# Two value groups of a decoder layer computed as one group of 1024 features

## The chip, the core and the metric

The kernel is one launch on one core of a Trainium2 chip. The metric is device time in microseconds (us) of the whole launch. Engines: PE is TensorE (matmuls), DVE is VectorE, ACT is ScalarE, POOL is GpSimd, SP is SyncE, which here issues most of the weight loads. DMAs can be issued from SP, ACT and POOL; those from SP and ACT go by the chip's hardware queues, those from POOL by a software queue.

## The reference

One layer of a decoder: 512 tokens, width 1024, float32. After an RMS norm, one input projection `h @ w_in` feeds two token mixers: gated linear attention (q, k, v, gate) and dilated attention in three groups of four heads with head width 128. The groups have dilations 1, 4 and 16, and their outputs are merged with weights made from their softmax sums:

```
for g, (win, dil) in enumerate(ATT_GROUPS):
    o_g, lse_g = dilated_attention(q_g, k_g, v_g, bias_g, dil, win // dil)
wts   = softmax(stack(lses), axis=0)
o_att = sum(wts[..., None] * stack(outs), axis=0)
```

Then come two merge gates, the output projection, an MLP with squared relu, and a gated projection of a side input. The change touches only the value projections of groups 1 and 2 (each 1024 x 512, here called v1 and v2), which need the tokens ordered by class: token t modulo 4.

## The kernel before, in words

**Precision and operands.** Every large product is made of three matmuls in a float32 form that TensorE takes rounded: hi x hi, hi x lo, lo x hi. A weight operand is a tile of 128 partitions x 1024; ACT rounds it to `hi` (L244), DVE subtracts to get `lo` (L239). Both tiles are padded, and those of the products below start at an offset of 32 elements (`SHIFT`).

**Products.** A projection of 512 features is done by Winograd's form of Strassen's scheme (`strassen`, L295 on): seven products of half size instead of eight. Its weight operands are A11, A12, A22 as loaded and S1 = A21 + A22, S2 = S1 + A11, S3 = A11 + A21, S4 = S2 + A12. S1 and S3 are made by a DMA that accumulates onto a loaded tile, issued by POOL (L210, L221; S3 over A11's tile, in place); S2 and S4 are DVE sums (L218, L224). For values the token tile is the stationary side and the weights are the moving side, 256 columns in each matmul; a product is four row pairs x two token halves x three matmuls = 24, so one group has 7 x 24 = 168 matmuls. Each product runs in one PSUM bank. After products 0 to 3 ACT copies a bank out (`begin`, L332); at the end DVE adds a later bank to that copy (`add`, L350).

**What sets the order.** Instructions are written out in program order, and every engine runs its own in that order. `fetch` keeps the preparation of operands a fixed number of operands ahead of the products: operand i+1 is rounded, i+2 summed, i+3 loaded (`prepare`), and S1's load and accumulation come 5 operands before A11 (`EARLY`). After every 8 matmuls `step` runs one queued evacuation from `later` and, when enough columns have passed (`pace`), one piece of a side generator from `side`. `drain` takes steps until both lists are empty, with no product between.

**Around the change.** While v1 and v2 run, the side generator `scores12` computes the scores of groups 1 and 2 (16 small matmuls for each of four heads, L704 and L705; softmax L683, L684, exponentials L688). Then it writes the softmax statistics to DRAM and reads them back in token order (L717, L719, both on POOL's queue), and PE transposes them (L723). `values_cls` brings values into class order the same way: four stores to `v_dram` (L662) and four strided reads back (L668) for each group, on POOL's queue. After v2 there is a `drain`; then v0 runs with `weights` as side generator. This makes the merge weights, and moves them through DRAM too (`k_dram` L770, `cc` L771, POOL). Then gq runs with `pv` as side generator, which multiplies probabilities by `cc` (L787), transposes them (L807, copied out L799) and multiplies them by v0 (L813, L815) and by v1 and v2 (L823, L824).

```
w = raw[f"{q}.S1"] = load(f"{q}.A21")
GP.dma_start(w, wts[UNIT[f"{q}.A22"]], accum_op=OP.add)      # L210
w = raw[f"{q}.S3"] = raw[f"{q}.A11"]
GP.dma_start(w, wts[UNIT[f"{q}.A21"]], accum_op=OP.add)      # L221
```

Of the kernel before, what the change touches and what calls it, by code (L numbers as in the profile page):

```python
# [10 lines left out]
F32 = mybir.dt.float32  # L11
# [3 lines left out]
OP = mybir.AluOpType  # L15
# [4 lines left out]
P = 128  # L20
# [14 lines left out]
def att_col(g, which):  # L35
    return ATT + (g * 3 + which) * 512


QUADS = ("quad", "quadt")


MLP2 = (("plain", 0, 0), ("seven", 0, 1), ("seven", 1, 1), ("plain", 0, 2), ("seven", 0, 3), ("seven", 1, 3),
# [4 lines left out]
def weight_units():  # L47

    u = []

    def fm(name, src, col, n, row=0):
        for j in range(n):
            u.append((f"{name}.{j}", "fm", src, row, col + j * P))

    def tm(name, src, col):
        for i in range(4):
            u.append((f"{name}.{i}", "tm", src, i * 2 * P, col))

    def quad(name, src, col, kind="quad", chunk=0):
        for m, k in ((0, 0), (1, 0), (1, 1), (0, 1)):  # L60
            u.append((f"{name}.A{m + 1}{k + 1}", kind, src, 2 * chunk + k, col + m * (P if kind == "quad" else 256)))

    fm("k0", "w_in", att_col(0, 1), 4)
    fm("q1", "w_in", att_col(1, 0), 4)
    quad("k1", "w_in", att_col(1, 1))
    quad("q2", "w_in", att_col(2, 0))
    quad("k2", "w_in", att_col(2, 1))
    quad("v1", "w_in", att_col(1, 2), "quadt")
    quad("v2", "w_in", att_col(2, 2), "quadt")
    quad("v0", "w_in", att_col(0, 2), "quadt")  # L70
    quad("gq", "w_in", GQ)
    quad("gk", "w_in", GK)
    quad("gv0", "w_in", GV, "quadt")
    for j in range(4):
        u.append((f"oa.{j}", "half", "w_o_attn", 0, j * 2 * P))
    quad("r0", "w_in", GR)
    quad("gv1", "w_in", GV + 512, "quadt")
    quad("r1", "w_in", GR + 512)
    for i in range(2):
        quad(f"gb{i}", "w_in", GATE + D + i * 512)  # L80
    for i in range(2):
        quad(f"ga{i}", "w_in", GATE + i * 512)
    fm("og", "w_o_gla", 0, 8)
    fm("wo", "w_out", 0, 8)
    for q in range(8):
        quad(f"m1q{q}", "w_mlp1", q * 512)
    for what, sub, c in MLP2:
        if what == "plain":
            for kk in range(4 * c, 4 * c + 4):
                u.append((f"m2s{sub}.{kk}", "tm", "w_mlp2", kk * 2 * P, sub * 512))  # L90
        else:
            quad(f"m2s{sub}c{c}", "w_mlp2", sub * 512, chunk=c)
    for j in range(2):
        u.append((f"pp{j}.0", "tm", "w_pp", 0, j * 512))
    for j in range(2):
        tm(f"pg{j}", "w_pg", j * 512)
    return u
# [13 lines left out]
BEGIN = {0: (((0, 0), "a"),), 1: (((1, 1), "c"),), 2: (((1, 0), "d"),), 3: (((0, 1), "a"),)}  # L111
END = {4: (((0, 0), "b"),), 5: (((0, 1), "c"),), 6: (((1, 1), "a"), ((1, 0), "a"))}

LEAD = 5


def operand_order():

    names = []
    for name, kind, *_ in UNITS:  # L120
        if kind not in QUADS:
            names.append(name)
        elif name.endswith("A11"):
            names += [f"{name[:-3]}{a}" for a, _, _ in STAGES]
    return names


OPERANDS = operand_order()
OPERAND = {n: i for i, n in enumerate(OPERANDS)}

EARLY = {max(i - LEAD, 0): n[:-4] for n, i in OPERAND.items() if n.endswith(".A11")}

C_LN2, C_LN3, C_BA, C_GN, C_LN1, C_LO, C_N = 0, 8, 16, 20, 28, 36, 38
W0, W12 = 384, 256
# [13 lines left out]
def block_kernel(ctx, tc, xT, ws, pT, wts, wha, wa2, vec, lnf, rel, onehot, ident_d, mask_d, out):  # L148
# [50 lines left out]
    def load(name):  # L199
        w = wst.tile([P, 1024], F32, tag="w", name="w")  # L200
        SY.dma_start(w, wts[UNIT[name]])
        return w

    def prepare(i):

        name = OPERANDS[i]
        if i in EARLY:
            q = EARLY[i]
            w = raw[f"{q}.S1"] = load(f"{q}.A21")
            GP.dma_start(w, wts[UNIT[f"{q}.A22"]], accum_op=OP.add)  # L210
        if name in UNIT:
            raw[name] = load(name)

    def sums(i):
        q, _, what = OPERANDS[i].rpartition(".")
        if what == "S2":
            w = raw[f"{q}.S2"] = raw[f"{q}.S1"]
            V.tensor_tensor(w, w, raw[f"{q}.A11"], op=OP.add)  # L218

            w = raw[f"{q}.S3"] = raw[f"{q}.A11"]  # L220
            GP.dma_start(w, wts[UNIT[f"{q}.A21"]], accum_op=OP.add)  # L221
        elif what == "S4":
            w = raw[f"{q}.S4"] = raw[f"{q}.S2"]
            V.tensor_tensor(w, w, raw[f"{q}.A12"], op=OP.add)  # L224

    def split_weights(tag, i, bufs):

        t = wsp.tile([P, 1024 + PAD], F32R, tag=tag, name=tag, bufs=bufs)
        o = SHIFT if OPERANDS[i] not in UNIT or UNITS[UNIT[OPERANDS[i]]][1] in QUADS else 0
        return t[:, o:o + 1024]  # L230

    def fetch(upto):
# [22 lines left out]
    def run(mms, n=PIECE, shared=False):  # L255
        for i in range(0, len(mms), n):
            for o, l, r, a, b in mms[i:i + n]:
                TE.matmul(o, lhsT=l, rhs=r, start=a, stop=b, skip_group_check=shared)  # L258
            step(PIECE * r.shape[-1])

    def three(ps, pairs):

# [38 lines left out]
    def strassen(name, xo, finish, tm=False, scale=1.0, extra=None, acc=None):  # L301

        bank, sums = {}, acc or {}

        def stage(op, xname, b):
            wh, wl = weight(f"{name}.{op}")
            fresh = b not in bank
            if fresh:  # L310
                bank[b] = mmt()
            mms = []
            for pr in range(4):
                xh, xl = xo(xname, pr)
                for n in range(2):
                    o = bank[b][:, halves(n)]
                    if tm:
                        c, r = slice(n * P, (n + 1) * P), slice(pr * 256, (pr + 1) * 256)
                        three = ((xh[:, c], wh[:, r]), (xl[:, c], wh[:, r]), (xh[:, c], wl[:, r]))
                    else:  # L320
                        c = slice((2 * pr + n) * P, (2 * pr + n + 1) * P)
                        three = ((wh[:, c], xh), (wh[:, c], xl), (wl[:, c], xh))
                    for i, (l, r) in enumerate(three):
                        mms.append((o, l, r, fresh and not mms, pr == 3 and i == 2))
            run(mms, shared=True)

        def begin(c, b):
            def go():
                if acc:
                    return add(c[0], sums[c], sums[c], bank[b])  # L330
                sums[c] = u32()
                S.activation(sums[c], bank[b], AF.Copy, scale=-scale if c[0] else scale)  # L332
            later.insert(0, go)

        def end(c, b):
            later.append(lambda: finish(*c, sums[c], bank[b]))

        for i, s in enumerate(STAGES):
            stage(*s)
            for c, b in BEGIN.get(i, ()):  # L340
                begin(c, b)
            for c, b in END.get(i, ()):
                end(c, b)
            if extra:
                extra(i)

    def add(m, out, s, ps, scale=1.0):

# [293 lines left out]
    def values(name, parts=False):  # L642
# [9 lines left out]
        strassen(name, xs_op, finish, tm=True)  # L652
        return res

    def values_cls(name):

        v_dram = dr.tile([T, 512], F32, name="v_dram")
        res, left = [], [4]

        def finish(m, t, s, ps):  # L660
            add(m, s, s, ps)
            GP.dma_start(v_dram[t * HT:(t + 1) * HT, m * HT:(m + 1) * HT].rearrange("(n p) c -> p n c", n=2),  # L662
                         s.rearrange("p (n c) -> p n c", n=2))
            left[0] -= 1
            if not left[0]:
                for c in range(4):
                    v = u32()
                    GP.dma_start(v, v_dram.rearrange("(m c) f -> c m f", c=4)[c])  # L668
                    res.append(v)

        strassen(name, xs_op, finish, tm=True)
        return res

    def softmax(ps, n0, bias, nm, sums, col, prob):
# [17 lines left out]
    st12 = const.tile([P, 2, 16], F32, name="st12")  # L692
    st0 = const.tile([P, 2, 16], F32, name="st0")
    sn = const.tile([P, 2, 16], F32, name="sn")
    p12, p0 = [], []

    def scores12():
        for h in range(4):
# [15 lines left out]
            yield  # L714

        s_dram = dr.tile([8, T], F32, name="s_dram")
        GP.dma_start(s_dram.rearrange("r (m c) -> m r c", c=4), st12.rearrange("p s (h c) -> p (s h) c", c=4))  # L717
        s_row = u32()
        GP.dma_start(s_row[0:32, 0:P], s_dram.rearrange("r (b t) -> (r b) t", b=4))  # L719
        for _ in range(6):  # L720
            yield
        pst = smt()
        TE.transpose(pst[:, 0:32], s_row[0:32, 0:P], ident[0:32, 0:32])  # L723
        yield
        V.tensor_copy(sn.rearrange("p a b -> p (a b)"), pst[:, 0:32])

    def scores0():
        for h in range(4):
# [14 lines left out]
    def weights():  # L743

        def small(name):
            return st.tile([P, 16], F32, tag=name, name=name, bufs=1)

        nmx, e0, e1, e2, dn, cn1 = (small(n) for n in ("nmx", "e0", "e1", "e2", "dn", "cn1"))
        V.tensor_tensor(nmx, st0[:, 0, :], sn[:, 0, :], op=OP.min)
        V.tensor_tensor(e0, nmx, st0[:, 0, :], op=OP.subtract)  # L750
# [272 lines left out]
    drain()  # L1023
    side.append(scores12())
    pace[0] = 3072
    v1 = values_cls("v1")
    v2 = values_cls("v2")
    drain()
    pace[0] = 2048
    side.append(weights())  # L1030
    v0 = values("v0")
# [479 lines left out]
def _layout(inputs):  # L1511
# [3 lines left out]
    for i, (_, kind, s, r, c) in enumerate(UNITS):  # L1515
# [2 lines left out]
            a = w[r:r + D, c:c + P].reshape(8, P, P).transpose(1, 0, 2)  # L1518
        elif kind == "tm":
            a = w[r:r + 2 * P, c:c + 512].reshape(2, P, 512).transpose(1, 0, 2)  # L1520
        elif kind == "quadt":

            a = w.reshape(4, 2, P, -1)[:, r, :, c:c + 256].transpose(1, 0, 2)
# [46 lines left out]
```

## Time and profile before

| | us |
|---|---|
| median of three runs | 964.02 (963.95 to 965.0) |
| profiled execution | 964.0 |
| its span on the core | 962.2 |
| PE busy | 954.1 |
| DVE busy | 743.2 |
| ACT busy | 538.2 |
| POOL busy | 103.6 |

The profiled execution is the span and 1.8 us around it. Its time is that of the median, so sums made on the trace can be set against the median as they are. Times in the views count from the start of the span. In the trace v1's products begin at 141.27, v2's at 168.49, v0's at 188.83 and gq's at 208.88. A busy PE is no proof of PE at its peak: the time from one matmul's start to the next (here: the cadence) says how fast it runs, and a matmul's own duration, which overlaps the next one, does not.

### The profile page before, as it was taken

The numbers are of one execution on the slowest core, as the hardware profiler recorded it, in microseconds if no ns is written. First come the engines' busy times: TensorE is split into PE (matmuls) and PEld (weight loads), VectorE is DVE, ScalarE is ACT, GpSimd is POOL, SyncE is SP. The second block draws the span as 40 slices with busy tenths as digits, with TensorE's granted clock in tenths as the row PEclk, the third lists the DMA queues.
The fourth block names the chain that finished last, engine by engine and source line by source line (L and its number), as shares of the span: only waits on it lengthen the run. The fifth ranks groups of instructions, "written<-read, shape, count | busy, mean of one in ns | idle before, by whom it ended". The sixth has DMA issues, their size and how long they took to land.

```text
span 962.2 us, 16747 instructions
## 1 busy us (share of the span) xinstructions
PE 954.1 (99%) x6734; PEld 894.2 (93%) x6734; DVE 743.2 (77%) x1064; ACT 538.2 (56%) x880; POOL 103.6 (11%) x145
## 2 busy tenths in 40 slices
PE   9999999999999999999999999999999999999997
PEld 8789999999998999999988899999998998988886
DVE  7688879676788769978856788777677899787754
ACT  7357547445657666675833446556665674354633
POOL 0140001420001021013010000011000100000000
PEclk9999999999999999999999999999999999999999
DMA  9385564964446555556536437565654464553102
GB/s 325 118 237 122 136 152 114 256 200 116 110 119 186 155 123 141 128 137 197 155 100 205 117 79 196 135 151 159 174 154 110 115 182 102 134 195 106 45 1 88
DMA packets 41326, 138.92 MB, mean 144 GB/s; under 512 B 5347, under 2 KB 5935, under 8 KB 41248
## 3 DMA queue, kind: packets, MB, share of 16 engines
q1 hardware_dynamic: 27648, 93.27, 29.2%
q0 software_dynamic: 12160, 42.20, 22.2%
q10 hardware_dynamic: 1440, 2.38, 0.7%
q8 instruction: 53, 0.87, 0.4%
q14 instruction: 25, 0.20, 0.1%
HBM read 131.50 MB, written 8.17 MB: 145 GB/s over the span
## 4 chain that ended last, share of the span: by engine, by line
PE 98%; DVE 1%; issue 1%; ACT 0%; POOL 0%; POOLq 0%; DVEq 0%; ACTq 0%
PE mmt L258 83%; PE smt L258 5%; PE mmt L480 2%; PE smt L867 1%; PE smt L807 1%; PE smt L732 1%; PE smt L452 0%; PE smt L824 0%; PE smt L705 0%; PE smt L813 0%; PE smt L704 0%; PE smt L823 0%; PE smt L995 0%; PE smt L1406 0%; PE smt L913 0%
## 5 line engine op out<-in xcount | busy, mean ns | idle before, releaser
L258 PE MATMUL mmt<-ur,hi 128*128 128x256 f32 (+1 forms) x3120 | 634.7, 301 | 0.0
L258 PEld LDWEIGHTS mmt<-ur,hi 128*128 128x128 f32 x3120 | 499.9, 188 | 21.6
L258 PE MATMUL mmt<-ur,lo 128*128 128x256 f32 (+1 forms) x1560 | 470.5, 302 | 0.0
L239 DVE TENSOR_TENSOR lo<-w,hi 128x1024 fp32r<-128x1024 f32 x250 | 303.1, 1219 | 50.3 <-PE mmt L258 32.4
L244 ACT ACTIVATE hi<-w 128x1024 fp32r<-128x1024 f32 x250 | 261.4, 1054 | 93.2 <-PE mmt L258 27.7
L258 PEld LDWEIGHTS mmt<-ur,lo 128*128 128x128 f32 x1560 | 293.8, 188 | 10.9
L258 PE MATMUL mmt<-hi,ur 128*128 128x256 f32 (+3 forms) x736 | 153.7, 306 | 0.0
L357 ACT ACTIVATE ur<-u 128x512 fp32r<-128x512 f32 x132 | 78.4, 624 | 104.4 <-DVE u L1107 30.9
L258 PEld LDWEIGHTS mmt<-hi,ur 128*128 128x128 f32 x736 | 118.5, 189 | 5.6
L350 DVE TENSOR_TENSOR u<-u,mmt 128x512 f32<-128x512 f32 (+1 forms) x124 | 78.3, 657 | 44.7 <-PE mmt L258 44.6
L258 PE MATMUL mmt<-lo,ur 128*128 128x256 f32 (+3 forms) x368 | 112.2, 305 | 0.0
L365 DVE TENSOR_TENSOR ur<-u,ur 128x512 fp32r<-128x512 f32 x131 | 86.3, 685 | 17.6 <-ACT ur L357 16.9
L332 ACT ACTIVATE u<-mmt 128x512 f32<-128x512 f32 x104 | 61.6, 592 | 55.8 <-PE mmt L258 55.5
L258 PEld LDWEIGHTS mmt<-lo,ur 128*128 128x128 f32 x368 | 69.4, 188 | 2.8
L221 POOL DMA_DIRECT2D w<-in_wts_dram x28 | 24.9, 888 | 360.6 <-DVE w L218 256.8
L210 POOL DMA_DIRECT2D w<-in_wts_dram x28 | 25.8, 920 | 273.1 <-DVE lo L239 66.0
L258 PE MATMUL smt<-ur,hi 128*128 128x512 f32 x160 | 50.4, 393 | 0.1
L258 PEld LDWEIGHTS smt<-ur,hi 128*128 128x128 f32 x160 | 29.8, 188 | 8.1 <-PE smt L562 0.8
L218 DVE TENSOR_TENSOR w<-w 128x1024 f32<-128x1024 f32 x28 | 34.3, 1225 | 1.0
L224 DVE TENSOR_TENSOR w<-w 128x1024 f32<-128x1024 f32 x28 | 34.3, 1225 | 1.0
L258 PE MATMUL smt<-ur,lo 128*128 128x512 f32 x80 | 31.2, 390 | 0.0
L390 ACT ACTIVATE u<-u 128x512 f32<-128x512 f32 x24 | 14.9, 622 | 16.7 <-DVE u L1188 16.7
(204 smaller groups left out, 714.5 us busy)
## 6 DMA issues: line engine op xcount, KB each, us to landing
w<-in_wts_dram SPq DMA_DIRECT2D x166, 512.0 KB, 4.4
w<-in_wts_dram POOLq DMA_DIRECT2D x56, 512.0 KB, 5.7
u<-in_xT_dram SPq DMA_DIRECT2D x8, 256.0 KB, 4.9
u<-in_ws_dram SPq DMA_DIRECT2D x8, 256.0 KB, 5.0
v_dram<-u POOLq DMA_DIRECT2D x8, 256.0 KB, 6.6
u<-v_dram POOLq DMA_DIRECT2D x8, 256.0 KB, 6.8
y_dram<-u ACTq DMA_DIRECT2D x8, 256.0 KB, 2.3
u<-y_dram POOLq DMA_DIRECT2D x8, 256.0 KB, 6.6
```

Of the source, the lines that this page charges most:

```text
L210: GP.dma_start(w, wts[UNIT[f"{q}.A22"]], accum_op=OP.add)
L218: V.tensor_tensor(w, w, raw[f"{q}.A11"], op=OP.add)
L221: GP.dma_start(w, wts[UNIT[f"{q}.A21"]], accum_op=OP.add)
L224: V.tensor_tensor(w, w, raw[f"{q}.A12"], op=OP.add)
L239: V.tensor_tensor(lo, w, hi.bitcast(F32), op=OP.subtract)
L244: S.activation(hi, w, AF.Copy)
L258: TE.matmul(o, lhsT=l, rhs=r, start=a, stop=b, skip_group_check=shared)
L332: S.activation(sums[c], bank[b], AF.Copy, scale=-scale if c[0] else scale)
L350: V.tensor_tensor(out, s, ps, op=OP.subtract if m else OP.add)
L357: S.activation(hi, x, AF.Copy)
L365: V.tensor_tensor(lo, x, hi.bitcast(F32), op=OP.subtract)
L480: TE.matmul(q0ps[i], lhsT=(hi, hi, lo)[j][:, c], rhs=(xh, xl, xh)[j], start=not k and not j, stop=k == KC - 1 and j == 2)
```

## The change

v1 and v2 become one group `v12` of 1024 features. Its scheme (`wide`, `WIDE`) has the same seven products, but in the order A11, S1, S2, A12, S3, S4, A22, and each has weights of 512 columns for each row pair (kind `quadw`): 24 matmuls of 512 columns where v1 and v2 had 24 of 256 each. A product uses two weight operands (`.0` and `.1`, two row pairs each) and two PSUM banks. Since `wide` calls `run` with 3, `step` comes after every 3 matmuls, and it is told 3 x 512 columns. The hi and lo tiles of these operands have no offset (`operand_kind`).

S3 is no longer made over A11: A11 is loaded a second time and A21 accumulated onto it, two operands before its own turn (`early`); S1 of `v12` and of the group behind it (v0) is loaded four operands before its turn, that of the other groups six, as before. ACT copies eight banks of 512 columns out, as many as before; two of the eight results come from one bank alone and are such copies (`whole`), so that DVE adds six times instead of eight.

Every class-ordered value tile is stored as [128 x 512] in two tensors `v0_dram` and `v1_dram`, one for each class group, and read back when its four stores are written. The statistics go to DRAM and back by ACT's queue (`S.dma_start`), with four side steps between the store and the read and five between the read and the transposition. The `drain` before v0 is gone: `weights` waits in the side list until the statistics are there (`sn_done`).

```diff
+WIDE = (("A11", "B11", "a"), ("S1", "T1", "c"), ("S2", "T2", "a"), ("A12", "B21", "b"), ("S3", "T3", "a"),
+        ("S4", "B22", "c"), ("A22", "T4", "a"))
+WBEGIN = {0: ((0, 0), "a"), 1: ((1, 1), "c"), 2: ((0, 1), "a")}
+WEND = {3: ((0, 0), "b"), 4: ((1, 1), "a"), 5: ((0, 1), "c"), 6: ((1, 0), "a")}
...
+        if what == "S1":
+            EARLY.setdefault(max(i - (4 if after_wide else 6), 0), []).append((n, f"{q}.A21", f"{q}.A22"))
...
+        elif what[:3] == "S1.":
+            EARLY.setdefault(i - 4, []).append((n, f"{q}.A21.{what[3:]}", f"{q}.A22.{what[3:]}"))
...
+        elif what[:3] == "S3.":
+            EARLY.setdefault(i - 2, []).append((n, f"{q}.A11.{what[3:]}", f"{q}.A21.{what[3:]}"))
...
-        o = SHIFT if OPERANDS[i] not in UNIT or UNITS[UNIT[OPERANDS[i]]][1] in QUADS else 0
+        o = SHIFT if operand_kind(OPERANDS[i]) in ("quad", "quadt") else 0
...
-            step(PIECE * r.shape[-1])
+            step(n * r.shape[-1])
...
+    def wide(name, xo, finish):
...
+            if fresh:
+                bank[b] = [smt() if b == "b" else mmt() for _ in range(2)]
+            for pr in range(4):
+                wh, wl = weight(f"{name}.{op}.{pr // 2}")
+                xh, xl = xo(xname, pr)
+                r = slice((pr % 2) * 512, (pr % 2 + 1) * 512)
+                mms = []
+                for n in range(2):
+                    c = slice(n * P, (n + 1) * P)
+                    for k, (l, w) in enumerate(((xh, wh), (xl, wh), (xh, wl))):
+                        mms.append((bank[b][n], l[:, c], w[:, r], fresh and not pr and not k, pr == 3 and k == 2))
+                run(mms, 3, shared=True)
...
+        def finish(m, t, n, s, ps):
+            s, r = whole(m, s, ps), (2 * t + n) * P
+            GP.dma_start(v_dram[m][r:r + P, :], s)
+            left[m] -= 1
+            if not left[m]:
                 for c in range(4):
                     v = u32()
-                    GP.dma_start(v, v_dram.rearrange("(m c) f -> c m f", c=4)[c])
-                    res.append(v)
+                    GP.dma_start(v, v_dram[m].rearrange("(m c) f -> c m f", c=4)[c])
+                    res[m].append(v)
...
-        GP.dma_start(s_dram.rearrange("r (m c) -> m r c", c=4), st12.rearrange("p s (h c) -> p (s h) c", c=4))
+        S.dma_start(s_dram.rearrange("r (m c) -> m r c", c=4), st12.rearrange("p s (h c) -> p (s h) c", c=4))
         s_row = u32()
-        GP.dma_start(s_row[0:32, 0:P], s_dram.rearrange("r (b t) -> (r b) t", b=4))
-        for _ in range(6):
+        for _ in range(4):
+            yield
+        S.dma_start(s_row[0:32, 0:P], s_dram.rearrange("r (b t) -> (r b) t", b=4))
+        for _ in range(5):
             yield
...
+        sn_done.append(True)
...
+        while not sn_done:
+            yield
...
-    v1 = values_cls("v1")
-    v2 = values_cls("v2")
-    drain()
+    v1, v2 = values_cls("v12")
```

PE at the start of v1 in the kernel before: pairs of hi and single lo products (`ur` is the token tile), then the first head's scores.

```order
L258 MATMUL mmt<-hi,ur 128x256 x2
L258 MATMUL mmt<-lo,ur 128x256
L258 MATMUL mmt<-hi,ur 128x256 x2
L258 MATMUL mmt<-lo,ur 128x256
L258 MATMUL mmt<-hi,ur 128x256 x2
L704 MATMUL smt<-u 128x128
L705 MATMUL smt<-u 128x128
```

The same place after the change:

```order
L296 MATMUL mmt<-ur,hi 128x256 x2
L296 MATMUL mmt<-ur,lo 128x256
L296 MATMUL mmt<-hi,ur 128x512 x2
L296 MATMUL mmt<-lo,ur 128x512
L785 MATMUL smt<-u 128x128
L786 MATMUL smt<-u 128x128
```

Every matmul of the projection has 512 columns instead of 256, and the scores stand at another place between them.

POOL in the kernel before, from v2's S3 (first L221) to the two accumulations behind `cc`. The two L210 make S1 of gq and of gk, the other L221 make S3 of v0 and of gq.

```order
L221 DMA w<-in_wts_dram 128x1024
L662 DMA v_dram<-u 128x2x256 x3
L668 DMA u<-v_dram 128x512 x4
L210 DMA w<-in_wts_dram 128x1024
L662 DMA v_dram<-u 128x2x256
L221 DMA w<-in_wts_dram 128x1024
L662 DMA v_dram<-u 128x2x256 x3
L668 DMA u<-v_dram 128x512 x4
L770 DMA k_dram<-u 16x128
L771 DMA cc<-k_dram 128x4x4
L210 DMA w<-in_wts_dram 128x1024
L221 DMA w<-in_wts_dram 128x1024
```

POOL after the change, from the first four stores to the same two accumulations (the two L244 make S1 of gq and of gk, the two L259 S3 of v0 and of gq):

```order
L744 DMA v_dram<-u 128x512 x4
L244 DMA w<-in_wts_dram 128x1024
L744 DMA v_dram<-u 128x512 x2
L749 DMA u<-v_dram 128x512 x4
L259 DMA w<-in_wts_dram 128x1024
L744 DMA v_dram<-u 128x512 x2
L749 DMA u<-v_dram 128x512 x4
L856 DMA k_dram<-u 16x128
L857 DMA cc<-k_dram 128x4x4
L244 DMA w<-in_wts_dram 128x1024
L259 DMA w<-in_wts_dram 128x1024
```

S3 of v0 stands behind the first class's four reads and ahead of the last two stores; before, it stood behind gq's S1 and one store, and three stores followed it. The two statistics DMAs are gone from this queue.

ACT after the change, around the statistics (L393 copies a bank out, L769 are the exponentials, L282 rounds weights):

```order
L393 ACTIVATE u<-mmt 128x512 x2
L769 ACTIVATE u,st_352<-u,st_352 128x256 x2
L798 DMA s_dram<-st_352 128x8x4
L282 ACTIVATE hi<-w 128x1024 x2
L393 ACTIVATE u<-mmt 128x512 x2
L802 DMA u<-s_dram 32x128
L282 ACTIVATE hi<-w 128x1024 x8
```

The store and the read of the statistics stand between the rounding of weights, four pieces of work apart.

## Rows read from the trace of the kernel before

**Rows 1.** The page: busy time and share by engine, then the ending chain by engine.
```profile
PE 954.1 (99%) x6734; PEld 894.2 (93%) x6734; DVE 743.2 (77%) x1064; ACT 538.2 (56%) x880; POOL 103.6 (11%) x145
...
PE 98%; DVE 1%; issue 1%; ACT 0%; POOL 0%; POOLq 0%; DVEq 0%; ACTq 0%
```

**Rows 2.** Waits of PE: line that waited, releaser, us; this is the whole answer.
```profile
PE smt L452 <- POOL ones L447: 1.0, 1, 1.0
```

**Rows 3.** Windows: stretch, us; busy us (count) by engine; PEclk, DMA share, GB/s.
```profile
141.27:188.83 47.56, 47.56 (x403) 47.38 (x402) 37.47 (x45) 26.58 (x54) 11.68 (x16) 1.00 0.70 184
...
168.49:188.83 20.34, 20.34 (x171) 20.16 (x170) 12.20 (x13) 9.59 (x11) 8.38 (x12) 1.00 0.97 271
```
```profile
143.58:162.00 18.42, 18.42 (x160) 18.42 (x159) 18.11 (x24) 13.80 (x39) 0.86 (x1) 1.00 0.52 126
```

**Rows 4.** Timeline of PE, 256 columns: start us, us, line, operands, count.
```profile
155.07 0.28 PE L258 MATMUL mmt<-lo,ur 128*128 128x256 f32 x1
155.19 0.39 PE L704 MATMUL smt<-u 128*128 128x128 f32 x2
...
156.89 0.49 PE L258 MATMUL mmt<-hi,ur 128*128 128x256 f32 x2
157.21 0.28 PE L258 MATMUL mmt<-lo,ur 128*128 128x256 f32 x1
...
161.53 0.28 PE L258 MATMUL mmt<-lo,ur 128*128 128x256 f32 x1
...
172.10 0.40 PE L258 MATMUL mmt<-hi,ur 128*128 128x256 f32 x2
...
172.45 0.40 PE L258 MATMUL mmt<-hi,ur 128*128 128x256 f32 x2
```

**Rows 5.** Timeline of PE, 512 columns, in the kernel's last products.
```profile
907.74 0.48 PE L258 MATMUL mmt<-hi,ur 128*128 128x512 f32 x1
908.05 0.39 PE L258 MATMUL mmt<-lo,ur 128*128 128x512 f32 x1
...
908.75 0.39 PE L258 MATMUL mmt<-lo,ur 128*128 128x512 f32 x1
...
925.34 0.39 PE L258 MATMUL mmt<-lo,ur 128*128 128x512 f32 x1
...
926.02 0.39 PE L258 MATMUL mmt<-lo,ur 128*128 128x512 f32 x1
```

**Rows 6.** Timeline of POOL: [idle before <-what ended it] at the end.
```profile
180.56 0.92 POOL L210 DMA_DIRECT2D w<-in_wts_dram  x1
...
186.96 0.89 POOL L221 DMA_DIRECT2D w<-in_wts_dram  x1 [1.91 <-issue]
...
190.56 1.44 POOL L662 DMA_DIRECT2D v_dram<-u  x2 [1.97 <-DVE u L350]
198.00 2.19 POOL L668 DMA_DIRECT2D u<-v_dram  x4 [5.99 <-issue]
200.18 0.52 POOL L770 DMA_DIRECT2D k_dram<-u  x1
209.47 0.79 POOL L771 DMA_DIRECT2D cc<-k_dram  x1 [8.78 <-DMA k_dram<-u]
...
210.82 1.26 POOL L221 DMA_DIRECT2D w<-in_wts_dram  x1
```

**Rows 7.** Tile s_dram: its issues on POOL, time to landing.
```profile
DMA to landing us min/median/max: 3.2/3.6/3.9
```

**Rows 8.** Tile v_dram: stores and reads, time to landing.
```profile
DMA to landing us min/median/max: 4.4/6.8/9.4
```

**Rows 9.** Timeline of ACT where gq.S3's weights land.
```profile
220.86 1.06 ACT L244 ACTIVATE hi<-w 128x1024 fp32r<-128x1024 f32 x1 [1.38 <-DMA w<-in_wts_dram]
...
222.31 1.56 ACT L799 ACTIVATE u<-smt 128x512 f32<-128x512 f32 x3
```

**Rows 10.** Timeline of PE at the same place.
```profile
225.38 0.61 PE L813 MATMUL smt<-u 128*128 128x128 f32 x4
```


## What the change should do to the time

> **What bounds the kernel now.** I read the page first: PE is busy for 954.1 us of a span of 962.2, and the chain that ended last is PE for 98% [rows 1]. The waits of PE come next: its only wait is 1.0 us at the very start [rows 2]. So no other engine and no transfer holds PE up, here or elsewhere, and a change can gain only PE's own time; whatever it moves on DVE, ACT, POOL or SP is worth nothing by itself and can only cost. The windows then give the stretch that is rewritten: v1 and v2 take 141.27 to 188.83, 47.56 us, with PE busy throughout at a granted clock of 1.00 (the 2.4 GHz level); the DMA engines are 0.70 busy over the whole and 0.97 in v2's part [rows 3]. The last view is PE's timeline, for the cadence, the time from start to start.
>
> **PE: half as many matmuls, each twice as wide.** Before there are 2 x 168 = 336 matmuls of 256 columns, after it 168 of 512, the same columns. In the second part of the stretch three matmuls start every 172.45 - 172.10 = 0.35 to 0.36 us (over many rows 0.356, so 0.1187 each); in the score stretch twelve groups of three take 161.53 - 157.21 = 4.32, 0.1200 each [rows 4]. Taking out the 16 matmuls of each head's scores (155.07 to 156.89 for all of 16 and the gap ahead, 1.82) and the longer gap behind them (157.21 - 156.89 = 0.32 for two, 0.20 and 0.12), the 47.56 leaves 38.86 for 326 plain gaps, 0.1192 on average.
> The trace has 512-column matmuls with weights moving and tokens standing at the kernel's end: 926.02 - 925.34 = 0.68 for three, 0.2267 each, and 908.75 - 908.05 = 0.70 (0.69 in the same place elsewhere), 0.230 each, soon after other work was let in; there the first gap is 908.05 - 907.74 = 0.31 [rows 5]. So the new cadence lies between 0.2267 and 0.230, against 2 x 0.1192 = 0.2384 for the same columns. I take 0.230 for about 60 of the 158 plain gaps (first half, where scores are let in and DVE is full) and 0.2267 for the rest, 0.2280 on average.
> Saved: about 163 pairs x (0.2384 - 0.2280) = 1.70. At the cheap end 163 x 0.0117 = 1.9, at the dear end (0.2305 throughout) 163 x 0.0079 = 1.3. The five insertions (four heads and the transposition of the statistics) cost as much as before: the gap behind one is longer by 0.08 at 256 columns and by 0.08 to 0.09 at 512, 0.05 in all at most. Sum on PE: -1.65, between -1.25 and -1.9.
> The Trainium skill ("TensorE: Matmul & The Clock Gate", Back-to-back issue gap) gives an isolated gap of N/2.4 + 2.5 ns, and a streamed figure for 512 columns well below that. By the first, 168 fewer matmuls would be worth 168 x 2.5 ns, an estimate of 0.4 us. The rows show more overhead for each matmul: 0.1192 at 256 columns is 12 ns over 256/2.4, and 0.2267 is 13 ns over 512/2.4, so the measured cadence decides.
>
> **Unshifted weights** are in that number, since the 512-column matmuls in [rows 5] read operands without an offset as well. For hi and lo themselves the shapes stay, so nothing.
>
> **DVE and ACT.** Fourteen weight operands are rounded and subtracted as before. DVE has six adds instead of eight. In the score stretch DVE is busy for 18.11 of 18.42 us [rows 3], and the new product order puts two S2 sums into it where one sum stood: one of 1.2 us more. It doesn't reach PE, as DVE works up to two operands ahead of the product: following the operands through, the tightest lo tile comes about 2 us before its product. If the cover were gone, PE would wait about 1 us once. I take 0, range 0 to 1.
>
> **Statistics by ACT's queue.** The two DMAs leave POOL. They landed 3.2 to 3.9 us after issue [rows 7]; with four side steps between store and read and five between read and transposition (3072 columns each, 1.4 us) the data is there some 4 us before PE wants it. ACT waits for the landing ahead of its read with two roundings queued behind it; ACT is busy for 26.58 of 47.56 us [rows 3] and has that slack. Cost 0, at most 0.5. Without `drain` PE does the same row of work, since nothing stood in it that PE waited for [rows 2]. 0.
>
> **SP.** Two loads of 512 KB more (A11 again, for S3). At the 271 GB/s of v2's part that is nearly 4 us of transfer [rows 3], in a stretch where the DMA share is 0.70. It delays what is on the queues, not PE directly.
>
> **POOL's queue, and what comes back.** This is the part that can cost. Before, POOL waited in turn for v1's stores, read them, accumulated for gq.S1 (180.56) and v0.S3 (186.96), stored v2's last two tiles at 190.56, read at 198.00, sent `k_dram` at 200.18 and, after 8.78 us of waiting for it, read `cc` at 209.47; gq.S3's accumulation went out right behind at 210.82 [rows 6]. After the change the first class's last stores can be written only after product six of seven (141.27 + 6/7 x 45.9 = 180.6, and about 1.5 for the adds: 182) and land 5 to 6 us later, so its four reads go out at 188 to 190, 8 us later than before, and v0.S3 stands behind them, at 190 to 192; landing 7 to 10 us later (gq.S3's took from 210.82 to 220.86 [rows 6, 9]) and split in 2.3, it is ready between 199 and 204; it is v0's last product, which begins at 206 less PE's gain, 204.3. It holds, at the late end with nothing to spare. The second class's stores then go out at 191 to 193.5, 0.5 to 1.5 later than before, the reads at 199 to 201, `k_dram` at about 201, and `cc` with gq.S3's accumulation between 208.5 and 211.2: a shift of -1 to +1.7, and 0.6 where I put it.
> PE meanwhile is at gq 1.65 earlier. Before, ACT waited 1.38 us for gq.S3's landing at 220.86, rounded it, and copied three transposed tiles out from 222.31, the second done at 223.35 [rows 9]; PE's next product of probabilities, which needs PSUM that these free, started at 225.38 [rows 10]. So 2.0 us were to spare, of which PE's gain takes 1.65. What is left is 0.35: PE stalls by what the shift has above that. At +0.6 that is 0.25, at +1.7 it is 1.35, at zero or less nothing.
>
> **Sum.** 964.0 (the profiled execution, which is at the median of the runs) - 1.65 + 0.25 = 962.6.
>
> **Rivals.** (A) All of the cadence and no stall: 964.0 - 1.9, with up to 0.4 more if the gaps behind the insertions shrink too, 961.7 to 962.1. For it: the clean 0.2267 in [rows 5] holds over long stretches. Against it: in the score stretch even 256 columns run at 0.1200 [rows 4], so something slows PE by a per cent there.
> (B) The cadence gives next to nothing: the overhead belongs to the columns or to what else runs, and 512 columns cost 2 x 0.118 here. The saving is then 163 x 0.0024 = 0.4, 963.6. [Rows 5] speak against it, in a stretch with little else running.
> (C) It ends slower: POOL's one queue is late. The stores of `v_dram` landed 4.4 to 9.4 us after issue, 6.8 in the middle [rows 8]; if the first class's last stores take 9.4 instead of 5.7, in a stretch where the DMA share was 0.97 already and now has 1 MB more [rows 3], then its reads, v0.S3, the second class's stores, `k_dram` and gq.S3 all come 3.7 later: a shift of about 4.3 and a stall of 4, net +2.3, 966.3. It decides from a shift of 2.0, where the gain is gone (`cc` at 211.5), and is measurably slower from 3.9 (`cc` after 213.4). For it: before, `k_dram` took 9 us for 8 KB behind four reads, so small things do wait behind large ones. Against it: the old order had v2's stores behind two accumulations and still met its time.
> The Trainium skill ("DMA: Bandwidth & Descriptors", Queues, rings and completion order) says that each DMA engine takes turns between the rows that have work. By it SP's extra loads slow POOL's stores but can't starve them, which leaves (C) possible and no more; the trace's 4.4 to 9.4 is of that kind.
>
> **Chances.** About 0.2% of 964, 1.93 us, is what a measurement of this kernel can tell from no change. My forecast (962.1 to 963.7, a saving below the clean one and a small stall) 0.46; A 0.21; B 0.08; a shift of 2 to 4, which lands within 0.2% of before (964 to 965.9), 0.08; C or another stall of that size (DVE's backlog and v0.S3 together) 0.17. Faster by over 0.2% is A and a little of the forecast's edge, 0.24; within it 0.59; slower 0.17. The likeliest case's own range is 962.1 to 963.7; with the bounds of POOL's queue it is 961.6 to 966.0, which leaves out the dear half of C.
>
> **What would show it.** Right: matmuls of the group 0.680 to 0.690 us apart by threes, about 45.9 us from its first to v0's first, no wait of PE in it, and `cc` read at 208.5 to 211.2 in the changed trace. A wait of PE at the transposition of the statistics would refute the ACT part, one ahead of the fourth product DVE's slack, one at v0's S3 or at `pv`'s products between 219 and 226 would be (C). Wrong altogether if the 512-column cadence is 0.236 or more, or if PE's waits grow above 2 us.

## The result and the profile after

The changed kernel takes 968.43 us (median of six runs, 966.22 to 969.61) against 964.15 (963.75 to 965.0): the ratio is 1.004, 95% interval 1.0029 to 1.005. It is slower by 4.3 us, where 962.6 was forecast and 966.0 was the upper end. The profiled execution took 967.88.

The page first (busy time by engine, then the chain that ended last). The chain was PE for 98% [rows 1]; now DMA, DVE, ACT and issue stand in it.

```profile
PE 954.8 (99%) x6566; PEld 887.2 (92%) x6566; DVE 742.7 (77%) x1062; ACT 538.2 (56%) x880; POOL 100.5 (10%) x143
...
PE 87%; DVE 5%; DMA 3%; issue 2%; ACT 2%; POOL 0%; POOLq 0%; DVEq 0%; ACTq 0%
```

The waits of PE say where. Before there was only the one at the start [rows 2]:

```profile
PE mmt L296 <- ACT u L370: 3.2, 1, 3.2
PE smt L525 <- POOL ones L520: 1.0, 1, 1.0
PE smt L893 <- ACT u L885: 0.2, 1, 0.2
```

The 3.2 us fall in v0, behind the rewritten stretch. PE's timeline (start us, duration us, line, operands) gives the stages: the first matmul of `v12`, two matmuls three apart near its end, and the first of v0.

```profile
141.46 0.63 PE L296 MATMUL mmt<-hi,ur 128*128 128x512 f32 x2
...
184.23 0.39 PE L296 MATMUL mmt<-lo,ur 128*128 128x512 f32 x1
...
184.91 0.39 PE L296 MATMUL mmt<-lo,ur 128*128 128x512 f32 x1
...
187.18 0.40 PE L296 MATMUL mmt<-hi,ur 128*128 128x256 f32 x2
```

`v12` takes 187.18 - 141.46 = 45.72 us where v1 and v2 took 47.56 [rows 3]: 1.84 gained. Three matmuls of 512 columns start every 184.91 - 184.23 = 0.68 us; the mean of the 157 plain gaps (those of two such matmuls with nothing let in between) is 0.2274. But v0, whose instructions for PE are the same as before, takes until 212.11: 24.93 us where it took 20.05 (188.83 to 208.88). That is 4.88 lost. The same timeline at v0's last product:

```profile
204.31 0.28 PE L296 MATMUL mmt<-lo,ur 128*128 128x256 f32 x1
207.74 0.80 PE L296 MATMUL mmt<-hi,ur 128*128 128x256 f32 x2 [3.15 <-ACT u L370]
...
208.55 0.63 PE L296 MATMUL mmt<-hi,ur 128*128 128x256 f32 x2
...
209.19 0.63 PE L296 MATMUL mmt<-hi,ur 128*128 128x256 f32 x2
...
211.04 0.40 PE L296 MATMUL mmt<-hi,ur 128*128 128x256 f32 x2
...
212.11 0.40 PE L296 MATMUL mmt<-ur,hi 128*128 128x256 f32 x2
```

PE stops behind 204.31 and starts again at 207.74, a gap of 3.43. Behind it, three matmuls of 256 columns take 209.19 - 208.55 = 0.64 us instead of 0.35, until about 211, and 0.35 again after that. The windows of this stretch (us; busy us and count of PE, PEld, DVE, ACT, POOL; granted clock; DMA share; GB/s) show why: the clock was granted at 0.50, the 1.2 GHz level, for some 3 us after the wait.

```profile
187.18:204.31 17.13, 17.13 (x146) 17.11 (x144) 5.87 (x11) 4.02 (x8) 4.17 (x7) 1.00 0.79 245
204.31:207.74 3.43, 0.28 (x4) 0.07 (x2) 1.74 (x2) 3.03 (x5) 0.22 (x1) 0.97 0.15 56
207.74:209.00 1.26, 1.26 (x6) 1.26 (x7) 1.26 (x3) 1.26 (x2) 1.26 (x3) 0.50 0.73 156
209.00:210.00 1.00, 1.00 (x6) 1.00 (x6) 1.00 (x2) 0.57 (x1) 1.00 (x3) 0.50 0.96 389
210.00:211.00 1.00, 1.00 (x7) 1.00 (x6) 0.97 (x2) 0.00 (x0) 0.16 (x1) 0.53 1.08 299
211.00:212.11 1.11, 1.11 (x11) 1.11 (x11) 1.04 (x2) 0.55 (x1) 0.00 (x0) 1.00 0.90 325
```

So the 4.88 are 3.3 of waiting (the gap less one ordinary start to start) and 1.5 of running at the lower clock; 0.05 lie ahead of the wait. PE's last matmul begins 4.04 us later than before. Of that, -1.84 + 4.88 = 3.04 arise in `v12` and v0, 0.56 in gq to gv0 (a wait of 0.2 on `pv`'s copies among them), 0.19 ahead of `v12` and 0.25 spread over the remaining 664 us.

What PE waited for is seen on ACT's and POOL's timelines. ACT first (the bracket is the idle time before, and what ended it):

```profile
193.23 0.60 ACT L370 ACTIVATE u<-mmt 128x512 f32<-128x512 f32 x1 [1.18 <-PE mmt L296]
204.71 1.06 ACT L282 ACTIVATE hi<-w 128x1024 fp32r<-128x1024 f32 x1 [10.88 <-DMA w<-in_wts_dram]
205.67 0.58 ACT L370 ACTIVATE u<-mmt 128x512 f32<-128x512 f32 x1
206.15 1.05 ACT L282 ACTIVATE hi<-w 128x1024 fp32r<-128x1024 f32 x1
207.10 0.59 ACT L370 ACTIVATE u<-mmt 128x512 f32<-128x512 f32 x1
```

The rounding of v0.S3's weights waited 10.88 us for its DMA. ACT works in order, and behind that instruction stood two copies of PSUM banks (L370); the second of them copies out the bank that v0's last product goes on adding to. It ended at 207.10 + 0.59 = 207.69, PE went on at 207.74. On POOL, which issued that DMA ([rows 6] show the queue before):

```profile
182.24 1.22 POOL L744 DMA_DIRECT2D v_dram<-u  x2 [1.09 <-DVE u L423]
191.80 2.13 POOL L749 DMA_DIRECT2D u<-v_dram  x4 [8.33 <-DMA v_dram<-u]
193.92 0.94 POOL L259 DMA_DIRECT2D w<-in_wts_dram  x1
194.48 1.48 POOL L744 DMA_DIRECT2D v_dram<-u  x2
207.52 2.14 POOL L749 DMA_DIRECT2D u<-v_dram  x4 [11.55 <-DMA v_dram<-u]
...
214.88 0.88 POOL L857 DMA_DIRECT2D cc<-k_dram  x1 [4.72 <-DMA k_dram<-u]
```

The first class's last two stores went out from 182.24 on and landed 7.9 and 8.3 us later (their data were in DRAM at 191.19); its reads had to wait until 191.80; v0.S3's accumulation stood behind them and was issued at 193.92 instead of 186.96. Everything behind came late too, `cc` at 214.88 instead of 209.47.

### The profile page after: what moved, and what is told of

Read it like the earlier page. It is cut to its first block, busy times and chain, and to the rows that moved or that the text cites. A ratio compares the mean times of both kernels' runs of the same rounds, so it can differ in the third digit from the quotient of the medians.

```text
span 966.1 us, 16417 instructions
## 1 busy us (share of the span) xinstructions
PE 954.8 (99%) x6566; PEld 887.2 (92%) x6566; DVE 742.7 (77%) x1062; ACT 538.2 (56%) x880; POOL 100.5 (10%) x143
## 4 chain that ended last, share of the span: by engine, by line
PE 87%; DVE 5%; DMA 3%; issue 2%; ACT 2%; POOL 0%; POOLq 0%; DVEq 0%; ACTq 0%
PE mmt L296 73%; PE smt L296 5%; PE mmt L553 2%; DMA w<-in_wts_dram 2%; DVE lo L277 2%; PE smt L953 1%; DMA v_dram<-u 1%; PE smt L893 1%; DVE ur L438 1%; PE smt L816 1%; ACT u L769 0%; PE smt L525 0%; ACT ur L430 0%; PE smt L910 0%; PE smt L899 0%
## 5 line engine op out<-in xcount | busy, mean ns | idle before, releaser
L282 ACT ACTIVATE hi<-w 128x1024 fp32r<-128x1024 f32 x250 | 261.3, 1054 | 105.4 <-PE mmt L296 24.5
L296 PEld LDWEIGHTS mmt<-ur,lo 128*128 128x128 f32 x1560 | 293.9, 188 | 10.8
L296 PE MATMUL mmt<-hi,ur 128*128 128x256 f32 (+3 forms) x608 | 144.8, 330 | 3.2 <-ACT u L370 3.2
L296 PEld LDWEIGHTS mmt<-hi,ur 128*128 128x128 f32 x608 | 103.0, 191 | 12.4 <-ACT u L370 3.4
L423 DVE TENSOR_TENSOR u<-u,mmt 128x512 f32<-128x512 f32 (+1 forms) x120 | 75.7, 657 | 37.3 <-PE mmt L296 37.2
L296 PE MATMUL mmt<-lo,ur 128*128 128x256 f32 (+3 forms) x304 | 99.8, 328 | 0.0
L370 ACT ACTIVATE u<-mmt 128x512 f32<-128x512 f32 x96 | 56.8, 592 | 50.9 <-PE mmt L296 50.6
L296 PEld LDWEIGHTS mmt<-lo,ur 128*128 128x128 f32 x304 | 57.9, 191 | 4.6
L259 POOL DMA_DIRECT2D w<-in_wts_dram x26 | 23.0, 886 | 360.9 <-DVE w L256 257.5
L244 POOL DMA_DIRECT2D w<-in_wts_dram x30 | 27.1, 928 | 291.7 <-DMA w<-in_wts_dram 105.5
L256 DVE TENSOR_TENSOR w<-w 128x1024 f32<-128x1024 f32 x26 | 31.9, 1226 | 0.9
L262 DVE TENSOR_TENSOR w<-w 128x1024 f32<-128x1024 f32 x26 | 31.9, 1225 | 0.9
```

Of the source, the lines that this page charges most:

```text
L244: GP.dma_start(w, wts[UNIT[b]], accum_op=OP.add)
L282: S.activation(hi, w, AF.Copy)
L423: V.tensor_tensor(out, s, ps, op=OP.subtract if m else OP.add)
```

## The experiments

Theory 1: what costs is the place of v0.S3's accumulation on POOL's queue, behind reads that wait for stores. Theory 2: the 1 MB of extra loads and the traffic of the stretch make every transfer late, whatever the order. A third reading, that the statistics part does it, has kernels of its own. Ratios are to runs of the kernel before on the same chip.

**Reads of the first class held until v0.S3 is issued** (`release` is called in `sums`, and after the second class's last store):

```diff
-                for c in range(4):
-                    v = u32()
-                    GP.dma_start(v, v_dram[m].rearrange("(m c) f -> c m f", c=4)[c])
-                    res[m].append(v)
+                held.append(lambda: reads(m))
+                if m:
+                    release()
...
             GP.dma_start(w, wts[UNIT[f"{q}.A21"]], accum_op=OP.add)
+            release()
```

> The changed kernel with one move on POOL's queue: the first class's four reads are held until v0.S3's accumulation has been issued (order: two stores, v0.S3, four reads, two stores, four reads, k_dram, cc). Theory 1 (place in the queue): the 3.2 us wait of PE in v0 and the 3.1 us at half clock behind it come from v0.S3's accumulation being issued at 193.9, behind the reads; issued at about 185 it lands before 196, v0 takes 20.0 us again instead of 24.9, and the time is 962.2 if gq doesn't stall instead; cc would be read at about 210 to 213, and PE may lose 0.2 to 3 us there, so 962.2 to 965. Theory 2 (bytes): the 1 MB of extra loads and the wide stores make every transfer late, whatever the order; v0.S3 still lands after 202 and the time stays at 966 to 969.

962.25 us, ratio 0.9981 (0.9972 to 0.999). PE's only wait is the one at the start; v0 takes 20.09. POOL:

```profile
185.71 0.90 POOL L265 DMA_DIRECT2D w<-in_wts_dram  x1 [2.12 <-DVE w L262]
191.27 2.16 POOL L761 DMA_DIRECT2D u<-v_dram  x4 [4.67 <-PE mmt L303]
...
208.61 0.79 POOL L869 DMA_DIRECT2D cc<-k_dram  x1 [3.98 <-DMA k_dram<-u]
```

One move takes 6 us off: v0.S3 landed 8.8 us after its issue, at 194.5. The bracket at the reads names PE; the stores that they read had landed only at 190.7. `cc` is read at 208.61, earlier than I expected for this order, and gq doesn't stall.

**All reads last** (as above, without the call in `sums`, so that the second class's stores go ahead of the reads as well).

> The changed kernel with all eight class-ordered reads behind the second class's last stores (order on POOL: two stores, v0.S3, two stores, eight reads, k_dram, cc). Theory 1 (place): v0.S3 is issued at about 185, the last stores at about 188.5 instead of 194.5, so the reads are out by 199, k_dram at about 199 and cc at 203 to 207, earlier than in the kernel before; no wait of PE in v0 nor in gq, and the whole 1.84 us that the wide group gains is kept: 962.2. Theory 2 (bytes): 966 to 969 as in the changed kernel.

961.93 us, ratio 0.998 (0.9971 to 0.9989): faster than the kernel before and the changed one, and not told apart from the variant above. PE's whole list of waits, and POOL:

```profile
PE smt L531 <- POOL ones L526: 1.0, 1, 1.0
```

```profile
185.28 0.90 POOL L265 DMA_DIRECT2D w<-in_wts_dram  x1 [2.12 <-DVE w L262]
187.29 1.24 POOL L750 DMA_DIRECT2D v_dram<-u  x2 [1.11 <-ACT e L850]
190.87 2.14 POOL L760 DMA_DIRECT2D u<-v_dram  x4 [2.34 <-DMA v_dram<-u]
...
204.90 0.80 POOL L868 DMA_DIRECT2D cc<-k_dram  x1 [5.97 <-DMA k_dram<-u]
```

The last stores go out at 187.29 instead of 194.48 and `cc` is read at 204.90, 4.6 ahead of the kernel before. The gain of `v12`, 1.84, is all there: 964.08 - 961.93 = 2.15. Theory 2 falls: the bytes are the same as in the changed kernel.

**The statistics part alone** (on the kernel before: `S.dma_start` with four and five steps, `sn_done`, no `drain`).

> The kernel before with the second part of the change alone: statistics to DRAM and back by ACT's queue, no drain ahead of v0; v1 and v2 as before. Theory 1 (place of v0.S3 behind reads, which only the wide group brings): nothing lands on PE's path, 963.5 to 964.5. Rival (ACT's queue or the missing drain holds ACT up, and bank copies with it): a wait of PE on ACT of 1 us or more and 965 to 968.

964.03 us, ratio 1.0 (0.9991 to 1.0008), no wait of PE. This part costs and gains nothing beside the old groups.

**The wide group alone** (on the changed kernel: statistics by `GP.dma_start` with six steps, `drain` ahead of v0).

> The first part of the change alone: the wide group, with the statistics by POOL's queue and the drain as before. Theory 1: v12 takes 45.7 us, v0.S3 stands behind the first class's reads as in the changed kernel, PE waits about 3 us in v0 and runs at half clock for some 3 us after it: 966 to 969. Rival (the statistics or the missing drain cause the wait): 962.2 to 963.

968.28 us, ratio 1.0039 (1.0026 to 1.0051). The time is as expected and the reason is not. PE's wait is at L804, the transposition of the statistics, and none is in v0:

```profile
PE smt L804 <- issue: 3.5, 1, 3.5
```

```profile
164.09 0.96 POOL L798 DMA_DIRECT2D s_dram<-st  x1 [13.40 <-ACT u L769]
168.61 0.54 POOL L800 DMA_DIRECT2D u<-s_dram  x1 [3.56 <-issue]
...
196.01 0.94 POOL L259 DMA_DIRECT2D w<-in_wts_dram  x1
```

The time that the two statistics DMAs took to land (tile `s_dram`), and ACT's rounding of v0.S3:

```profile
DMA to landing us min/median/max: 4.0/4.5/5.0
```

```profile
203.91 1.06 ACT L282 ACTIVATE hi<-w 128x1024 fp32r<-128x1024 f32 x1 [4.97 <-DMA w<-in_wts_dram]
```

PE stopped after a matmul that began at 169.85 and transposed at 173.73. POOL sent the statistics out at 164.09 and read them back from 168.61; with 5.0 us to land the read was there at 173.6, just ahead of the transposition. `v12` with that wait and the lower clock behind it takes 50.87 instead of 45.72; v0 starts 5 us later, and so its S3, issued at 196.01 and landed at 203.8, is in time for once. So the wide group needs the second part of the change, and what looked like an ornament removed a wait that the wide group would bring. Which piece of that part does it is not shown: in the changed kernel ACT's read landed by 170.5, 3 us sooner, but nine side steps instead of six also put PE's transposition at 174.62 instead of 170.1, late enough for POOL's 173.6 as well.

**Reads in their place, from data that are ready** (bytes and order stay, the wait goes):

```diff
-                    GP.dma_start(v, v_dram[m].rearrange("(m c) f -> c m f", c=4)[c])
+                    GP.dma_start(v, (v_dram[m] if m else xT[0:T, :]).rearrange("(m c) f -> c m f", c=4)[c])
```

> The changed kernel, with the first class's four reads in their place on POOL's queue, of the same size and stride, but from the input x, which is in DRAM from the start; so v1's values are rows of x here, not values. POOL no longer waits for the stores at that place, and the bytes ahead of v0.S3's accumulation stay. Theory 1a (the wait for the stores holds the queue up): the reads go out at about 183.5, v0.S3 at about 186, it lands before 198, PE doesn't wait in v0, 962 to 963. Theory 1b (the 1 MB of reads ahead of the accumulation in the queue makes it late): it takes 10 us or more to land even so, and as the second class's stores are late too, some wait of PE stays; 964 or more.

962.11 us, ratio 0.9983 (0.9974 to 0.9992); PE doesn't wait. POOL's reads and accumulation, and ACT's rounding of v0.S3 (its idle time ended by that DMA):

```profile
183.08 1.60 POOL L749 DMA_DIRECT2D u<-in_xT_dram  x3
...
186.18 0.90 POOL L259 DMA_DIRECT2D w<-in_wts_dram  x1 [0.75 <-DVE e L837]
```

```profile
196.59 1.06 ACT L282 ACTIVATE hi<-w 128x1024 fp32r<-128x1024 f32 x1 [3.14 <-DMA w<-in_wts_dram]
```

With the 1 MB of reads ahead of it the accumulation took 10.3 us to land, about as long as in the changed kernel (10.7) and 1.5 more than with the reads behind it (8.8 in the first experiment). So the long landing that 1b expected did come, but the wait and the time that it expected did not, and 1a holds: the issue 8 us later, because POOL sat at a wait, is what made it late. The 1.5 is no fixed price of the reads: in the wide group alone the same four reads stood right ahead of the accumulation, and it landed in 7.8.

**A late v0.S3 in the kernel before** (v1 and v2 as two groups):

```diff
-            GP.dma_start(w, wts[UNIT[f"{q}.A21"]], accum_op=OP.add)
+            go = lambda: GP.dma_start(w, wts[UNIT[f"{q}.A21"]], accum_op=OP.add)
+            held.append(go) if q == "v0" else go()
...
+                if name == "v2":
+                    held.pop()()
```

> The kernel before, with one move: v0.S3's accumulation is issued behind v2's four reads, at about 200 instead of 187. Nothing of the wide group is in it. If a late v0.S3 is by itself what costs, PE waits at v0's last product: landing at 208 to 211 and 2.3 us for hi and lo against a start at 206 give a wait of 4 to 7 us, then some 3 us at the lower clock level, about 1.5 us more: 969 to 973. If the wide group's own traffic is needed for the loss, 964 to 965.

972.01 us, ratio 1.0083 (1.0069 to 1.0097).

```profile
PE mmt L261 <- ACT u L335: 5.5, 1, 5.5
```

```profile
196.57 2.16 POOL L671 DMA_DIRECT2D u<-v_dram  x4 [4.79 <-DMA v_dram<-u]
198.72 0.93 POOL L223 DMA_DIRECT2D w<-in_wts_dram  x1
```

A wait of 5.5 us on the same bank copy and then some 5 us at the lower clock, which cost 2.4: gq's first matmul comes at 216.80 instead of 208.88. Nothing of the wide group is in it.

**S3 of `v12` in place** (no extra loads; two lines of `early` out, three into `sums`):

```diff
-        elif what[:3] == "S3.":
-            EARLY.setdefault(i - 2, []).append((n, f"{q}.A11.{what[3:]}", f"{q}.A21.{what[3:]}"))
...
+            if what[1] == "2":
+                w = raw[f"{q}.S3{what[2:]}"] = raw[f"{q}.A11{what[2:]}"]
+                GP.dma_start(w, wts[UNIT[f"{q}.A21{what[2:]}"]], accum_op=OP.add)
```

> The changed kernel with v12's S3 made in place over A11, as the other groups make it: the two extra loads of 512 KB are gone, the order on POOL around the reads and v0.S3 is the changed kernel's. Theory 1 (place in the queue): PE still waits about 3 us in v0 and the time stays at 966 to 969. Theory 2 (bytes): with 1 MB less in the stretch v0.S3 lands in time, 962 to 963.

967.58 us, ratio 1.0035 (1.0014 to 1.0055), with the same wait at the same place; v0.S3 was issued at 193.75:

```profile
PE mmt L297 <- ACT u L371: 3.2, 1, 3.2
```

The extra megabyte is not the cause. The runs spread from 964.42 to 969.81, as those of the changed kernel do; that such a time varies with the landing of a DMA is likely, but one trace of each kernel doesn't show it.

**All reads last, with the offset of 32 elements on `v12`'s tiles** (one word: `operand_kind(...) in ("quad", "quadt", "quadw")`).

> The variant with all reads last (961.93), with v12's hi and lo tiles at the offset of 32 elements that the other products have. If the offset is without effect on 512-column matmuls, as I assumed, 962.0 within 0.4 and a cadence of 0.68 to 0.69 us for three; if the unshifted tiles carry part of the gain, v12 takes more than 45.7 us and the time is 962.5 to 964.

962.48 us, ratio 0.9987 (0.9979 to 0.9996). First matmul of `v12`, two matmuls three apart, first of v0:

```profile
141.98 0.63 PE L302 MATMUL mmt<-hi,ur 128*128 128x512 f32 x2
...
184.82 0.40 PE L302 MATMUL mmt<-lo,ur 128*128 128x512 f32 x1
...
185.52 0.39 PE L302 MATMUL mmt<-lo,ur 128*128 128x512 f32 x1
...
188.54 0.39 PE L302 MATMUL mmt<-hi,ur 128*128 128x256 f32 x2
```

Three matmuls take 0.70, the mean gap is 0.2323 instead of 0.2274, and `v12` takes 46.56 instead of the 45.72 of the changed kernel and of four of its variants. The offset is not without effect: without it the 512-column matmuls run 2% faster, worth 0.84 us here. That is read from the traces; the ratios of the two variants to the kernel before overlap. It also splits the gain: with the offset on both sides, half as many matmuls of twice the width are worth 47.56 - 46.56 = 1.00 us, and dropping the offset gives the other 0.84. Whether 256-column matmuls without the offset would have gained as much by themselves no run shows.

## Why the prediction was wrong

**What held.** PE was the bound, and the gain of the cadence was sized well: 1.65 forecast (1.25 to 1.9), 1.84 measured. The cadence I took was 0.2280 on average and came out at 0.2274. What it stands for was only half right: its rows were of unshifted tiles and those of 256 columns of shifted ones, so 0.84 of the 1.84 is the offset, which the prediction counted in without a price of its own, and 1.00 is the halved number of matmuls. The isolated gap that the Trainium skill gives ("TensorE: Matmul & The Clock Gate", Back-to-back issue gap), by which an estimate of 0.4 us would be gained, does not fit that 1.00 either. DVE and the extra loads cost PE nothing, and the statistics landed in time by ACT's queue:

```profile
DMA to landing us min/median/max: 2.8/3.2/3.5
```

**The step that failed** is the one on v0.S3: "ready between 199 and 204 ... It holds, at the late end with nothing to spare." It was ready at 207.0 and PE at 207.7. Three terms of it were too small. The last stores of the first class were given 5 to 6 us to land and took 7.9 and 8.3, so the reads went out at 191.80 instead of 188 to 190 and the accumulation at 193.92 instead of 190 to 192. [rows 8], on which that term could rest, mixes stores and reads: its 4.4 and 9.4 are both reads, and its eight stores took 5.3 to 7.4, so even the trace of before had stores above 6. Then the accumulation took 10.7 where I allowed 7 to 10. And hi and lo were the only work that I put behind the landing; lo was made on DVE:

```profile
205.80 1.23 DVE L277 TENSOR_TENSOR lo<-w,hi 128x1024 fp32r<-128x1024 f32 x1 [10.97 <-ACT hi L282]
```

The bank copies that stand behind the rounding on ACT were overlooked: the order of ACT's queue decides, and PE waited for the copy, 0.7 us longer than for lo.

**The price.** I counted a wait at its own length. The 3.3 us of idle PE were followed by some 3 us at the 1.2 GHz level, 1.5 us more; the trace of before, where PE never waits, has no row for that, and I gave it no bound.

**The rival.** (C) named the mechanism, late stores that push all of POOL's queue back, and the prediction's own sign for it, a wait of PE at v0's S3, came; `cc` did come at 214.88, past the 213.4 from which it should decide. The forecast's bounds were drawn too narrow here: last stores at 191 to 193.5 are 0.4 to 2.9 later than the 190.56 of [rows 6], not 0.5 to 1.5. It was priced at gq's products, 966.3. There PE waited only 0.2, since v0 had already held it up for longer: here the late chain was paid for at its first place. The chance of 0.17 was too low for a chain whose own rows, [rows 8] and [rows 6], left nothing to spare at the late end.

The Trainium skill ("DMA: Bandwidth & Descriptors", Queues, rings and completion order) was read as a reason why POOL's stores couldn't be held up for long. It speaks of another thing, how packets of several queues share the DMA engines, which no run here tests. What the runs show is that POOL's instructions are issued in order, and a read that waits for a semaphore keeps an independent accumulation from being issued at all (193.92 against 186.18 with ready data).

## What to carry to other kernels

Where an engine issues DMAs in order, a DMA that waits for data must stand behind every DMA that doesn't and that someone needs soon; here one such move turned 968.4 into 962. When a transfer is late, look at everything queued behind the instruction that waits for it, copies out of PSUM above all, and price PE's wait with the lower clock behind it, about half as much again for 3 us. When a product gets faster or is finished in another order, work out again when each side transfer is wanted: with the wide group, PE came to the statistics 3.5 us before POOL's queue had them, and to v0.S3 more than 3 us before its copies were done.

## What the runs showed of the hardware

After waits of 3.2, 3.5 and 5.5 us (the changed kernel, the wide group alone, the late v0.S3) PE ran at a granted clock of 0.50 for about 3, 3 and 5 us, at a cost of about 1.5, 1.5 and 2.4 us. An offset of 32 elements in the moving operand (and its hi and lo tiles alike) made 512-column matmuls 2% slower, 0.2323 against 0.2274 us. The accumulating DMA of 512 KB for v0.S3, from POOL's queue, took 7.0 us to land in the kernel before and 7.8 to 10.8 in the others; with 1 MB of reads right ahead of it 7.8 to 10.8, without them 7.0 to 8.9. In every trace all of POOL's DMAs (118 to 120) landed in the order of their issue, so a small one waits for large ones ahead of it: in the kernel before `k_dram`, 8 KB, took 9.0 us behind four reads of which the last landed 0.15 us before it.
